# Hybrid layer on one core: the last attention pair ahead of the gate in program order, and half of the gate ahead of the second value group

## The chip, the cores and the metric

The kernel runs on one core of a Trainium2 chip. The metric is device time in microseconds of one launch; several launches are timed, and their median counts. TensorE (PE) multiplies matrices, VectorE (DVE), ScalarE (ACT) and GpSimd (POOL) do elementwise work, and SyncE (SP) issues most of the DMAs.

## The reference

One residual layer over 1024 tokens of width 1024, all in float32. A single projection feeds two groups of heads that run beside each other; their outputs are joined, projected and added to the input, and a mixture of 16 experts follows.

```python
xn = rms_norm(h, attn_norm[l])
u = xn @ w_in[l]
o_a = hgrn2_mixer(u[..., o0:o1], u[..., o1:o2], u[..., o2:o3], u[..., o3:o4], lb_all[l], hg_norm[l])
o_b = fox_mixer(u[..., o4:o5], u[..., o5:o6], u[..., o6:o7], u[..., o7:IN_COLS], fox_f_bias[l], fox_norm[l])
h = h + jnp.concatenate([o_a, o_b], axis=-1) @ w_out[l]
h = h + hier_moe(rms_norm(h, ffn_norm[l]), ...)
return rms_norm(h, final_norm)
```

`hgrn2_mixer` is a gated linear recurrence with 4 heads of width 128; its output is normalized and multiplied by `silu(g_raw)`, the gate that this change moves. `fox_mixer` is causal softmax attention with a cumulative forget bias, 8 heads of width 64.

## The kernel before, in words

Every float32 product is made of three matmuls of rounded halves (`mm3`, lines 248 to 251): hi by hi, lo by hi, hi by lo. The lo half is what the rounding to the hi half left over. ACT makes the hi half by a cast, and DVE or POOL the lo half by a subtraction.

The mixer is written out by hand as a list of calls, and a scheduler then sets each engine's order. It takes an instruction as soon as its inputs are ready by its own estimate, and among several the one that comes first in program order. So a call that is written later is a filler: its matmuls go where the earlier call leaves the engine free. What it puts out is a fixed order for each engine, and on the chip an engine waits at an instruction that is not ready, with all that is queued behind it.

The calls are these. `hg_v(p)` projects the values of two recurrent heads, `hg_fq(h)` their forget gates and queries, and `hg_core(h)` is the recurrence: seven levels of small score matmuls (line 504), with DVE and POOL work between them (lines 507 to 523). `fox_v(g)` projects the attention values of four heads, two pairs (192 matmuls of 128x256 for the second group). `fox_kq(p)` projects keys and queries of pair p, one projection each. `fox_core(p)` runs `fox_steps(p)`, a generator: for each of four blocks of 256 queries and both heads it makes two rows of scores (`row`: lines 379 to 383 on PE, the reduction L384 on DVE, the exponential L388 on ACT) and then attends over the block before (`attend`: the transposes L401, the cast `ph` L406 on ACT, the subtraction `pl` L407 on DVE, the matmuls L411 and L412). `collect` copies the sum out (L432), transposes it (L435) and reduces it (L437); after every second block `finish` normalizes four token tiles with small DVE operations (L115 to L121, L420 to L423) and two POOL multiplications (L419, L426), and stores them to `o_d` (L427).

`hg_g(p)` projects one half of the gate: 192 matmuls of 128x256, for each of 8 token tiles a tanh on ACT (L571), a product on DVE (L572) and a store to `g_d` (L573). Its tile `sg` has two buffers, so the third tanh waits for the first store. `piece` loads a stretch of `w_in`.

In program order pair 3 ends the mixer: `hg_core(3)`, `hg_g(0)`, then 18 of the 36 steps of pair 3, then `hg_g(1)`, and then the other 18 steps by hand between parts of the output projection. `prep(k)` (L621, L622) splits one of eight slices of the output weights; its target lies where the normalized input `XH`, `XL` was, so it can begin only when the last gate matmul has read that. `front_a(i)` loads one tile of mixer output (`om` from `o_d`) and gate (`gm`, or `he` for the first tile), multiplies them (L636), transposes (L642) and splits them (L645, L646). `front_parts(i)` is a generator over the 48 matmuls of one output tile (`bk<-wohi,ohi`), with an addition L666 behind each half. Two limits hold the order there: each `prep` cast is issued after the last `ph` cast written so far (`LF['act']`), and three groups of three output matmuls of tile 0 each after the last attention transpose written so far (`LF['tr']`). Then follow routing (`back`) and the experts.

Of the kernel before, what the change touches and what calls it, by code (L numbers as in the profile page):

```python
# [80 lines left out]
def build(ctx, tc, x, attn_norm, w_in, hg_lb_logits, hg_norm, fox_f_bias, fox_norm, w_out, ffn_norm,  # L81
# [197 lines left out]
    def fox_v(g):  # L279
        ts = [rtile("fv") for _ in range(4)]  # L280
        for q in range(4):
            FV[4 * g + q] = ts[q].rearrange("p (j c) -> p j c", j=NT)

        def ev(b, i):
            for q in range(4):
                v = FV[4 * g + q][:, i]
                A.copy(v[:, 0:64], b[:, q * 64:(q + 1) * 64])
                V.tensor_sub(v[:, 64:128], b[:, q * 64:(q + 1) * 64], v[:, 0:64].bitcast(F32))
            if not g:
                V.tensor_add(ff[:, :, i], b[:, 256:264], fb_bc)  # L290
        proj_t(3072 + 256 * g, 256 if g else 264, ev, None if g else 3584)
# [4 lines left out]
    def fox_kq(p):  # L296
        ka, kb, qa, qb, ql, qm = (rtile(n) for n in ("ka", "kb", "qa", "qb", "ql", "qm"))
        kl = up.tile([128, S], F32R, name="kl", tag="L", bufs=4)

        lo_, up_ = slice(0, 64), slice(64, 128)  # L300

        def ev_k(b, sl):
            for hi, h, o in ((ka, lo_, up_), (kb, up_, lo_)):
                A.copy(hi[h, sl], b[h])
                V.tensor_sub(kl[h, sl], b[h], hi[h, sl].bitcast(F32))  # L305
                mv(hi[o, sl], kl[h, sl])

        def ev_q(b, sl):
            for hi, lo, h, o in ((qa, ql, lo_, up_), (qb, qm, up_, lo_)):
                A.activation(hi[h, sl], b[h], AF.Copy, scale=-0.125)  # L310
                mv(hi[o, sl], hi[h, sl])
                V.scalar_tensor_tensor(lo[h, sl], b[h], -0.125, hi[h, sl].bitcast(F32), op0=OP.mult, op1=OP.subtract)
                mv(lo[o, sl], lo[h, sl])
        proj_c(2560 + 128 * p, ev_k)
        proj_c(2048 + 128 * p, ev_q)
        out = (((qa, ka), (ql, ka)), ((qb, kb), (qm, kb)))
        FS[p] = out
# [32 lines left out]
    LF = {}  # L350
# [107 lines left out]
    def fox_core(p):  # L458
        for _ in fox_steps(p):
            pass  # L460
# [13 lines left out]
    def hg_fq(h):  # L474
        F, K, Q = utile("hF"), utile("hK"), utile("hQ")
        HF[h], HK[h], HQ[h] = F, K, Q

        def ev_f(b, sl):
            A.activation(F[:, sl], b, AF.Tanh, scale=0.5)
            G.tensor_scalar(F[:, sl], F[:, sl], lb[:, 1, h:h + 1], lb[:, 0, h:h + 1], op0=OP.mult, op1=OP.add)  # L480
            G.tensor_scalar(K[:, sl], F[:, sl], -0.5, 0.5, op0=OP.mult, op1=OP.add)

        def ev_q(b, sl):
            A.activation(Q[:, sl], b, AF.Tanh, scale=0.5)
            V.scalar_tensor_tensor(Q[:, sl], Q[:, sl], 1.0, b, op0=OP.add, op1=OP.mult)

        proj_c(512 + 128 * h, ev_f)
        proj_c(128 * h, ev_q)
# [79 lines left out]
    def hg_g(p):  # L568
        def ev(b, i):
            z = up.tile([128, 256], F32, name="sg", tag="sg", bufs=2)  # L570
            A.activation(z, b[:, 0:256], AF.Tanh, scale=0.5)  # L571
            V.scalar_tensor_tensor(z, z, 1.0, b[:, 0:256], op0=OP.add, op1=OP.mult)  # L572
            nc.sync.dma_start(g_d[i * 128:(i + 1) * 128, 256 * p:256 * p + 256], z)  # L573
        proj_t(1536 + 256 * p, 256, ev)
# [12 lines left out]
    fox_core(1)  # L587
    hg_v(1)
    hg_core(2)
    fox_v(1)  # L590
    fox_kq(2)
    fox_core(2)
    hg_fq(3)
    fox_kq(3)
    hg_core(3)
    hg_g(0)
    steps = fox_steps(3)
    for _ in range(18):
        next(steps, None)
    hg_g(1)  # L600
    w_out_v = w_out.rearrange("l (k p) c -> p (l k) c", p=128)
    raws = []
# [13 lines left out]
            WOH.append(wh_[:, k])  # L616
            WOL.append(wl_[:, k])

    def prep(k, lim=True):
        with (tc.issue_after(LF['act'].ins) if lim else nullcontext()):  # L620
            A.copy(WOH[k], raws[k])  # L621
        (G, V)[k in (2, 5)].tensor_sub(WOL[k], raws[k], WOH[k].bitcast(F32))  # L622

    oa_cm = tc.tile_pool(name="oa", bufs=2, reuse_waits="tile")
# [45 lines left out]
        for _ in front_parts(i):  # L670
            pass

    next(steps, None)
    next(steps, None)
    prep(0)
    next(steps, None)
    next(steps, None)
    prep(1)
    next(steps, None)
    prep(2)  # L680
    next(steps, None)
    next(steps, None)
    prep(3)
    next(steps, None)
    front_a(0)
    front_a(1)
    prep(4)
    next(steps, None)
    next(steps, None)
    prep(5)  # L690
    next(steps, None)
    prep(6)
    next(steps, None)
    next(steps, None)
    prep(7)
    next(steps, None)
    next(steps, None)
    next(steps, None)
    fr0 = front_parts(0)
    with tc.issue_after(LF['tr'].ins):  # L700
        for _ in range(3):
            next(fr0, None)
    next(steps, None)
    with tc.issue_after(LF['tr'].ins):
        for _ in range(3):
            next(fr0, None)
    next(steps, None)
    with tc.issue_after(LF['tr'].ins):
        for _ in range(3):
            next(fr0, None)  # L710
    for _ in steps:
        pass
    for _ in fr0:
        pass
    ps_cm.__exit__(None, None, None)
    ps_cm = tc.tile_pool(name="pt", bufs=1, space=PSUM, reuse_waits="tile")
    ps = ps_cm.__enter__()
# [636 lines left out]
```

## Time and profile before

| | us |
|---|---|
| median of 3 runs | 1112.72 |
| lowest and highest of the runs | 1109.21, 1117.45 |
| the profiled execution, its own time | 1116.4 |
| its span, first to last instruction | 1114.6 |
| PE busy in the span | 1050.8 |
| DVE busy | 684.8 |
| ACT busy | 499.5 |
| POOL busy | 366.9 |

The profiled execution lies 3.7 us above the median of the runs, and 1.8 us of it are outside its span. Pair 0 of the attention begins at 133 us of the span, pair 1 at 261, pair 2 at 381 and pair 3 at 483; the gate's last matmul is at 544.7, and routing begins at about 601. A busy PE says little by itself: matmuls overlap, and at half clock the same work fills twice the time. So the granted clock is read beside it.

### The profile page before, as it was taken

To read this page: it belongs to the slowest core of one execution; us is meant where nothing else is said; L and a number is where in the kernel's file an instruction comes from. 1 tells how busy PE (TensorE), PEld (TensorE's weight loads), DVE (VectorE), ACT (ScalarE), POOL (GpSimd) and SP (SyncE) were. 2 spreads that over 40 slices of the span, in tenths; PEclk is the share of its full clock that TensorE was granted. 3 is DMA by queue.
4 is the path that set the end of the run, shared out by engine and by line. 5 is a ranking of instruction groups with operands and counts; after the bars stand their busy time and mean duration, and the time that the engine had idled before them with its cause. 6 is when DMAs were issued, how large, how long until landed. Compare 5 with 4: busy or idle time off the path is not lost. (4 is left out here: it accounts for less than half of the span.)

```text
span 1114.6 us, 19354 instructions
## 1 busy us (share of the span) xinstructions
PE 1050.8 (94%) x7471; PEld 891.2 (80%) x7471; DVE 684.8 (61%) x1616; ACT 499.5 (45%) x861; POOL 366.9 (33%) x283
## 2 busy tenths in 40 slices
PE   6999999989999999899899899699999999999994
PEld 6989788869988887789777788576777778878793
DVE  4537546655575546844654576656778778777445
ACT  5423343324443333424441233465666667667341
POOL 2024123221032112410322233334655456545312
PEclk8999999989999998999979999699999999999998
DMA  7120611112121410281307942369989999999974
GB/s 243 39 58 21 151 41 48 58 38 76 31 66 30 123 48 20 62 250 40 122 30 235 361 167 76 120 225 374 370 315 329 347 322 377 298 319 374 305 285 167
DMA packets 103967, 193.98 MB, mean 174 GB/s; under 512 B 9852, under 2 KB 43756, under 8 KB 103872
## 3 DMA queue, kind: packets, MB, share of 16 engines
q1 hardware_dynamic: 92576, 169.98, 43.9%
q0 software_dynamic: 7568, 20.96, 7.5%
q10 hardware_dynamic: 3728, 1.77, 0.6%
q8 instruction: 60, 0.98, 0.4%
q14 instruction: 35, 0.29, 0.1%
HBM read 155.85 MB, written 30.68 MB: 167 GB/s over the span
## 5 line engine op out<-in xcount | busy, mean ns | idle before, releaser
L249 PE MATMUL bk<-whi,xhi 128*128 128x256 f32 (+1 forms) x384 | 112.3, 292 | 4.0 <-ACT whi L178 2.8
L1053 DVE TENSOR_TENSOR wl<-we,wh 128x1024 fp32r<-128x1024 f32 x64 | 91.9, 1445 | 35.7 <-ACT wh L1051 34.9
L251 PE MATMUL bk<-whi,xlo 128*128 128x256 f32 (+1 forms) x384 | 110.6, 288 | 0.2 <-DVE xlo L216 0.2
L250 PE MATMUL bk<-wlo,xhi 128*128 128x256 f32 (+1 forms) x384 | 109.5, 285 | 1.1 <-DVE wlo L179 1.1
L250 PE MATMUL ch<-wl,xh 128*128 128x512 f32 (+1 forms) x336 | 109.4, 326 | 0.0
L1051 ACT CAST wh<-wm 128x1024 fp32r<-128x1024 f32 x84 | 87.3, 1049 | 48.3 <-PE ch L251 45.4
L251 PE MATMUL ch<-wh,xl 128*128 128x512 f32 (+1 forms) x336 | 108.3, 324 | 0.0
L249 PE MATMUL ch<-wh,xh 128*128 128x512 f32 (+1 forms) x336 | 108.2, 329 | 0.0
L249 PE MATMUL bk<-xhi,whi 128*128 128x512 f32 x256 | 104.0, 406 | 2.6 <-DVE kl L305 2.4
L1051 ACT CAST wh<-we 128x1024 fp32r<-128x1024 f32 x84 | 87.2, 1049 | 41.2 <-PE ch L251 41.0
L1053 DVE TENSOR_TENSOR wl<-wm,wh 128x1024 fp32r<-128x1024 f32 x63 | 92.9, 1504 | 17.4 <-ACT wh L1051 17.4
L251 PE MATMUL bk<-xhi,wlo 128*128 128x512 f32 x256 | 103.4, 404 | 0.0
L250 PE MATMUL bk<-xlo,whi 128*128 128x512 f32 x256 | 102.8, 401 | 0.0
L249 PEld LDWEIGHTS bk<-whi,xhi 128*128 128x128 f32 x384 | 73.1, 190 | 5.7 <-ACT whi L178 3.1
L406 ACT CAST ph<-ch 128x512 fp32r<-128x512 f32 (+1 forms) x80 | 43.1, 542 | 75.9 <-PE ch L401 75.7
L1053 POOL TENSOR_TENSOR wl<-we,wh 128x1024 fp32r<-128x1024 f32 x20 | 51.1, 2553 | 73.7 <-ACT wh L1051 73.7
L250 PEld LDWEIGHTS bk<-wlo,xhi 128*128 128x128 f32 x384 | 73.4, 191 | 1.8 <-DVE wlo L179 1.6
L251 PEld LDWEIGHTS bk<-whi,xlo 128*128 128x128 f32 x384 | 73.3, 191 | 0.7 <-DVE xlo L216 0.4
L250 PEld LDWEIGHTS ch<-wl,xh 128*128 128x128 f32 x336 | 64.9, 193 | 9.1 <-issue 4.1
L249 PEld LDWEIGHTS ch<-wh,xh 128*128 128x128 f32 x336 | 64.5, 194 | 8.0 <-ACT xh L1065 1.6
L407 DVE TENSOR_TENSOR pl<-ch,ph 128x512 fp32r<-128x512 f32 (+1 forms) x80 | 50.3, 633 | 33.3 <-ACT ph L406 33.2
L1053 POOL TENSOR_TENSOR wl<-wm,wh 128x1024 fp32r<-128x1024 f32 x21 | 52.0, 2476 | 53.7 <-ACT wh L1051 53.6
(423 smaller groups left out, 2639.6 us busy)
## 6 DMA issues: line engine op xcount, KB each, us to landing
we<-in_w_gate_dram SPq DMA_DIRECT2D x8, 2048.0 KB, 20.0
we<-in_w_up_dram SPq DMA_DIRECT2D x8, 2048.0 KB, 18.3
we<-in_w_down_dram SPq DMA_DIRECT2D x8, 2048.0 KB, 17.9
wm<-in_w_gate_dram SPq DMA_DIRECT2D x8, 2048.0 KB, 8.3
wm<-in_w_up_dram SPq DMA_DIRECT2D x8, 2048.0 KB, 10.9
wm<-in_w_down_dram SPq DMA_DIRECT2D x8, 2048.0 KB, 14.7
wraw<-in_w_in_dram SPq DMA_DIRECT2D x26, 512.0 KB, 4.3
xt<-in_x_dram SPq DMA_DIRECT2D x8, 512.0 KB, 14.8
```

The lines of the kernel that those rows point to most:

```text
L249: T.matmul(o, l[0], r[0], start=first, stop=False)
L250: T.matmul(o, l[0], r[1], start=False, stop=False)
L251: T.matmul(o, l[1], r[0], start=False, stop=last)
L406: LF['act'] = A.copy(ph[:, :o], b[:, :o])
L407: V.tensor_sub(pl[:, :o], b[:, :o], ph[:, :o].bitcast(F32))
L1051: A.copy(hi, src)
L1053: (G if j % 3 == 2 else V).tensor_sub(lo, src, hi.bitcast(F32))
```

## The change

Four things move in the list of calls, and no computation is added or taken away. The gate's first half `hg_g(0)` goes from behind `hg_core(3)` up to the place ahead of `fox_v(1)`. `hg_core(3)` goes ahead of `fox_kq(3)`. All 36 steps of pair 3 go ahead of `hg_g(1)`, as a plain `fox_core(3)`. And the hand-made end goes: the eight `prep` calls, `front_a(0)`, `front_a(1)` and `front_b(0)` simply follow, with no limits on when they are issued. Lines behind 590 move up by 3, and from the end of `prep` on by 3 and later by 40.

```diff
     hg_core(2)
+    hg_g(0)
     fox_v(1)
     fox_kq(2)
     fox_core(2)
     hg_fq(3)
+    hg_core(3)
     fox_kq(3)
-    hg_core(3)
-    hg_g(0)
-    steps = fox_steps(3)
-    for _ in range(18):
-        next(steps, None)
+    fox_core(3)
     hg_g(1)
...
-    def prep(k, lim=True):
-        with (tc.issue_after(LF['act'].ins) if lim else nullcontext()):
-            A.copy(WOH[k], raws[k])
+    def prep(k):
+        A.copy(WOH[k], raws[k])
         (G, V)[k in (2, 5)].tensor_sub(WOL[k], raws[k], WOH[k].bitcast(F32))
...
-    next(steps, None)
-    next(steps, None)
-    prep(0)
...
+    for k in range(8):
+        prep(k)
     front_a(0)
     front_a(1)
...
-    fr0 = front_parts(0)
-    with tc.issue_after(LF['tr'].ins):
-        for _ in range(3):
-            next(fr0, None)
-    next(steps, None)
...
+    front_b(0)
```

On ACT, behind the gate's last tanh (L571), the casts of the output weights (`wohi`) stand between the attention's exponentials (`Lg,fls`) and casts (`ph`). Before, from the last tanh:

```order
L571 ACTIVATE sg<-bk 128x256
L406 CAST ph<-ch 128x512
L621 CAST wohi_5704<-woraw 128x1024
L406 CAST ph<-ch 128x384
L621 CAST wohi_5704<-woraw 128x1024 x2
L406 CAST ph<-ch 128x512
L388 ACTIVATE Lg,fls<-Lg,mn 128x896
L406 CAST ph<-ch 128x512
L621 CAST wohi_5704<-woraw 128x1024
L645 ACTIVATE ohi<-bk,hgn 128x512
L645 ACTIVATE ohi<-bk,fxn 128x512
L388 ACTIVATE Lg,fls<-Lg,mn 128x1024
```

and now, from the same tanh:

```order
L571 ACTIVATE sg<-bk 128x256
L618 CAST wohi_5969<-woraw 128x1024 x4
L618 CAST wohi_5971<-woraw 128x1024 x2
L388 ACTIVATE Lg,fls<-Lg,mn 128x640
L406 CAST ph<-ch 128x512
L618 CAST wohi_5971<-woraw 128x1024 x2
L406 CAST ph<-ch 128x384
L388 ACTIVATE Lg,fls<-Lg,mn 128x768
L388 ACTIVATE Lg,fls<-Lg,mn 128x896
L388 ACTIVATE Lg,fls<-Lg,mn 128x1024
```

Six casts now stand in one run ahead of the next exponential, and the multiplications' split of `front_a(0)` (`ohi`) stands behind the last exponential, further down.

On PE, in the last steps of pair 3, `bk<-wohi,ohi` are the output matmuls of tile 0, `ub` the attention's sums. Before, in the middle of the last attention blocks:

```order
L251 MATMUL bk<-wohi_5704,olo 128x512
L411 MATMUL ub<-ph,fv 128x256
L412 MATMUL ub<-pl,fv 128x256
L411 MATMUL ub<-ph,fv 128x256
L412 MATMUL ub<-pl,fv 128x256
L401 MATMUL ch<-cft,Lg 128x128 x4
L249 MATMUL bk<-wohi_5704,ohi 128x512
L250 MATMUL bk<-wolo_5705,ohi 128x512
L251 MATMUL bk<-wohi_5704,olo 128x512
```

and now, at their very end:

```order
L411 MATMUL ub<-ph,fv 128x256
L412 MATMUL ub<-pl,fv 128x256
L411 MATMUL ub<-ph,fv 128x128
L412 MATMUL ub<-pl,fv 128x128
L435 MATMUL ch<-cft,ut 128x128 x4
L639 MATMUL bk<-cft,om 128x128 x8
L249 MATMUL bk<-wohi_5969,ohi 128x512
L250 MATMUL bk<-wolo_5970,ohi 128x512
```

The output matmuls stood between the attention's last blocks; now they stand behind all of them, behind the collect (`ch<-cft,ut`) and behind the transposes of `front_a(1)` (L639, before L642).

On PE, in pair 2, `hc<-hQ,hK` are the scores of `hg_core(3)` and `bk<-xhi,whi` and its like the first projection of `fox_kq(3)`. Before, the last projection matmuls and the first scores:

```order
L249 MATMUL bk<-xhi_75,whi 128x512
L250 MATMUL bk<-xlo_76,whi 128x512
L251 MATMUL bk<-xhi_75,wlo 128x512
L504 MATMUL hc<-hQ,hK 64x64 x12
L435 MATMUL ch<-cft,ut 128x128 x4
L401 MATMUL ch<-cft,Lg 128x128 x4
L504 MATMUL hc<-hQ,hK 64x64 x4
L411 MATMUL ub<-ph,fv 128x256
L401 MATMUL ch<-cft,Lg 128x128 x4
L504 MATMUL hc<-hQ,hK 64x64 x16
```

and now, where the first 8 scores are through:

```order
L401 MATMUL ch<-cft,Lg 128x128 x3
L379 MATMUL rb<-kb,qb 128x512
L381 MATMUL rb<-kb,qm 128x512
L504 MATMUL hc<-hQ,hK 64x64 x7
L250 MATMUL bk<-xlo_74,whi 128x512
L251 MATMUL bk<-xhi_73,wlo 128x512
L379 MATMUL rb<-kb,qb 128x128
L381 MATMUL rb<-kb,qm 128x128
L383 MATMUL rb<-mskr,idr 128x128
L249 MATMUL bk<-xhi_73,whi 128x512
```

The first set of 16 scores now stands inside the projection, where it stood behind it. On DVE, which the rows don't show, two subtractions of output weights and nine small operations of `finish` now stand between the reductions L384 right behind the gate's last tanh; the multiplication of `front_a(0)` (`om<-om,he`) stands behind the last L384, and that of `front_a(1)` behind the last reduction L420.

## Rows read from the trace of the kernel before

**Rows 1.** The page: the span, and TensorE's granted clock in 40 slices
```profile
span 1114.6 us, 19354 instructions
...
PEclk8999999989999998999979999699999999999998
```

**Rows 2.** Busy time in five stretches: us busy (instructions), PEclk, DMA share, GB/s
```profile
core 0: us, PE busy (x) PEld busy (x) DVE busy (x) ACT busy (x) POOL busy (x), PEclk, DMA share, GB/s
261.00:298.00 37.00, 37.00 (x310) 36.53 (x309) 17.81 (x57) 17.84 (x48) 4.71 (x6) 1.00 0.16 44
...
427.00:472.00 45.00, 38.61 (x418) 32.72 (x417) 40.00 (x88) 19.56 (x36) 19.71 (x21) 0.92 0.16 48
483.00:545.00 62.00, 60.79 (x509) 59.97 (x508) 29.38 (x95) 22.66 (x53) 5.58 (x6) 1.00 0.39 123
545.00:589.00 44.00, 36.54 (x196) 30.80 (x194) 26.60 (x44) 22.81 (x36) 14.21 (x6) 0.84 0.26 84
589.00:601.00 12.00, 11.34 (x50) 8.93 (x48) 4.80 (x22) 0.00 (x0) 3.13 (x4) 1.00 0.53 128
```

**Rows 3.** Timeline of PE, the gate's last matmuls: start, us, what, waits
```profile
542.82 0.28 PE L250 MATMUL bk<-wlo,xhi 128*128 128x256 f32 x1
...
544.70 0.28 PE L251 MATMUL bk<-whi,xlo 128*128 128x256 f32 x1
```

**Rows 4.** Timeline of PE, two waits behind the gate
```profile
552.55 1.09 PE L642 MATMUL bk<-cft,om 128*128 128x128 f32 x8 [2.61 <-DVE om L636]
...
556.64 0.44 PE L379 MATMUL rb<-kb,qb 128*128 128x384 f32 x1 [2.41 <-DVE mn L384]
```

**Rows 5.** Timeline of DVE in the last stretch
```profile
549.73 2.77 DVE L636 TENSOR_TENSOR om<-om,he 128x512 f32<-128x512 f32 x1 [1.05 <-DMA he<-g_d]
...
553.03 2.89 DVE L622 TENSOR_TENSOR wolo<-woraw,wohi 128x1024 fp32r<-128x1024 f32 x1
...
563.76 1.21 DVE L622 TENSOR_TENSOR wolo<-woraw,wohi 128x1024 fp32r<-128x1024 f32 x1
```

**Rows 6.** Timeline of POOL in the same stretch
```profile
541.10 1.04 POOL L426 TENSOR_TENSOR OF<-OF,fls 128x512 f32<-128x512 f32 x1 [5.13 <-DVE fls L121]
547.24 4.70 POOL L622 TENSOR_TENSOR wolo<-woraw,wohi 128x1024 fp32r<-128x1024 f32 x2 [5.10 <-ACT wohi L621]
```

**Rows 7.** Timeline of SP's queue and its loads at pair 3's start
```profile
480.82 3.20 SPq L605 DMA_DIRECT2D woraw<-in_w_out_dram  x5
...
490.33 0.33 SPq L573 DMA_DIRECT2D g_d<-sg  x1
```

**Rows 8.** Timeline of ACT there
```profile
498.97 0.38 ACT L571 ACTIVATE sg<-bk 128x256 f32<-128x256 f32 x1 [6.33 <-DMA g_d<-sg]
```

**Rows 9.** Timeline of ACT: output weights' casts, last exponential, last casts
```profile
547.46 2.00 ACT L621 CAST wohi<-woraw 128x1024 fp32r<-128x1024 f32 x2
...
565.88 1.16 ACT L388 ACTIVATE Lg<-Lg,mn 128x1024 f32<-128x1024 f32 x1
...
571.36 0.59 ACT L406 CAST ph<-ch 128x512 fp32r<-128x512 f32 x1 [1.25 <-PE ch L401]
...
574.98 0.59 ACT L406 CAST ph<-ch 128x512 fp32r<-128x512 f32 x1 [0.57 <-PE ch L401]
```

**Rows 10.** Timeline of PE around the first output tile's projection
```profile
574.70 0.49 PE L249 MATMUL bk<-wohi,ohi 128*128 128x512 f32 x1
...
588.57 0.60 PE L435 MATMUL ch<-cft,ut 128*128 128x128 f32 x4
589.51 0.50 PE L249 MATMUL bk<-wohi,ohi 128*128 128x512 f32 x1 [0.35 <-DVE he L666]
```

**Rows 11.** Timeline of DVE after the last collect
```profile
589.37 0.75 DVE L437 TENSOR_REDUCE OF<-ch 128x128 f32<-128x256 f32 x2
591.34 0.69 DVE L420 TENSOR_REDUCE fls<-fsq 128x8 f32<-128x512 f32 x1 [1.22 <-POOL fsq L419]
```

**Rows 12.** Group of DVE, 427 to 472: busy us, mean ns, idle
```profile
L508 DVE TENSOR_TENSOR hQ<-hQ,hF 128x1024 f32<-128x1024 f32 x1 | 1.8, 1781 | 0.0
```

More of the change, by code (lines that the diff above doesn't have):

```diff
@@ L671, in front_b @@
             pass
-    next(steps, None)
-    next(steps, None)
-    prep(0)
-    next(steps, None)
[L677 to L684, printed above, removed]
+    for k in range(8):
+        prep(k)
     front_a(0)
     front_a(1)
[L687 to L698, printed above, removed]
-    fr0 = front_parts(0)
-    with tc.issue_after(LF['tr'].ins):
-        for _ in range(3):
-            next(fr0, None)
[L703 to L714, printed above, removed]
+    front_b(0)
     ps_cm.__exit__(None, None, None)
```

## The prediction

> **What bounds the kernel now.** I read the page first: the span is 1114.6 us, and TensorE's granted clock is high in most slices, with a few low ones [rows 1]. So PE sets the end nearly everywhere, and a change of order can only gain or lose where PE waits or where its clock falls. Since the change moves work between stretches of the mixer, I then read the busy times by stretch [rows 2]. In the first half of pair 1 (261 to 298 us) PE is busy all of 37.0 us at full clock. In the first half of pair 3 (483 to 545), which holds both halves of the gate, it is busy 60.8 of 62.0. Both are bound by matmuls. Two stretches are not. In the second half of pair 2 (427 to 472) DVE is busy 40.0 of 45.0 and PE 38.6 at a mean clock of 0.92: DVE's work sets the pace. In the tail behind the gate (545 to 589) PE is busy 36.5 of 44.0 at a mean clock of 0.84. A mean of 0.84 between full and half speed is (1 - 0.84) x 2 x 44 = 14 us at 1.2 GHz. Here nothing is full: ACT has 22.8 us of work and DVE 26.6. This is a chain of scores, reduction, exponential, transposes, cast and sums, and PE waits for it. The prediction hangs on these two stretches.
>
> **The first part: half of the gate changes places with the second value group.** Each is 192 matmuls of 128x256. The gate's last 17 start from 542.82 to 544.70, so one takes (544.70 - 542.82) / 16 = 0.1175 us [rows 3], and 192 take 22.6. Beside pair 1's end the gate's half stands where the values stood, with the same count of matmuls: no difference. The values then run by themselves ahead of pair 2, which moves all of pair 2 back by 22.6 us, and pair 3 has 22.6 us less to cover: 62.0 - 22.6 = 39.4 us for its first half. These cancel if 39.4 us are enough for the chain. Pair 1's first half is the test: it holds 192 matmuls of one projection beside the same attention steps, and takes 37.0 [rows 2]. So I could give 2.4 us back, but pair 3 has something that pair 1 lacks. Its gate products leave through `g_d`, and the first store is issued at 490.33, behind output weights of which the first five loads alone are issued from 480.82 on [rows 7]. The third tanh waited 6.33 us for it, and ran at 498.97 [rows 8]. Before, PE had whole gate tiles queued and hardly noticed. Now attention steps stand between the gate's matmuls, and a `ph` cast stands right behind that tanh. But the third tanh also comes later by itself: two tiles beside attention steps take longer than two tiles alone, so that I take some 2.5 us of the wait as seen by PE. Sum of this part: 0, with -2.4 as the lower end and +6.3 (all of the wait) as the upper.
>
> **The second part: the recurrence core ahead of the last keys and queries.** One set of 16 scores of seven moves from behind the first projection into it. Behind the first set stands the product L508, 1.8 us on DVE [rows 12], which is then done while PE is covered by a projection; with the sum of 40.0 in 45.0 us, DVE time taken out shortens the stretch about one for one. Gain 2 us, 4 if the second set's work follows it. Against it: the core's last matmuls stood among the second projection and the start of pair 3, and now stand ahead of that projection, with state updates of DVE between them. I take 1 us for them. Sum -1 us, from -4 to +1.
>
> **The third part: the tail.** Its start is the gate's last matmul at 544.7 [rows 3], and the same attention steps are left then as before: five rows' ends and three attention blocks of head 0, then all the rest. I go through it in order.
>
> Up to the last exponential the old kernel takes 565.88 + 1.16 - 544.7 = 22.3 us [rows 9]. In it PE waited 2.61 us for the product of `front_a(0)` and then 2.41 us for a reduction that was queued behind it on DVE [rows 4]. Both go, since that product now stands behind the last reduction: -5. New is the run of six casts on ACT, ahead of an exponential that is ready: two such casts take 2.00 us [rows 9], six take 6. Five of the eight subtractions come at once on POOL, two of them take 4.70 us [rows 6], five 11.8. DVE's part beside them grows: a subtraction of output weights took 2.89 us while POOL was at its own, and 1.21 otherwise [rows 5], 1.7 us more. DVE has two such subtractions and nine small operations of `finish` between the last reductions; ACT's run and DVE's waits lie largely beside each other, so I take 3 us of both, with 0 (all beside) and 5 x 1.7 = 8.5 (one wait for each POOL subtraction) as ends. That gives 22.3 - 5 + 3 = 20.3.
>
> The Trainium skill, SBUF — State Buffer, section Who interferes with whom, says that a VectorE instruction with two inputs in SBUF and a GpSimd instruction that reads SBUF exclude each other for the whole of an instruction. The trace agrees (2.89 against 1.21 us). By that rule alone each POOL subtraction of 2.35 us could hold one DVE operation, 11.8 us in place of the 3 that I take.
>
> `finish` of the first half now ends late: its last product on POOL stands behind five subtractions, so at 12 to 15 us after the gate's end. From the end of that product before, at 541.10 + 1.04 = 542.14 [rows 6], to the start of the product of `front_a(0)` at 549.73 [rows 5], store, load and landing took 7.6 us. So that product can start only at 20 to 23 us, and in DVE's order the last collects and subtractions stand behind it. I take 2.7 us beyond the 20.3: 23.
>
> Then come eight attention blocks, which follow each other in (574.98 - 571.36) / 3 = 1.21 us [rows 9]; one is begun by then, seven take 8.5: 31.5. Before, from 574.70 to 588.57 the last of these blocks were spread between the 48 matmuls of output tile 0 [rows 10], and PE worked on one while the other waited. Now all 48 stand behind the last block, the collect, and the transposes of `front_a(1)`. Collect: copy and transposes, about 1.6. Then DVE: from 588.57, when the collect's transposes begin [rows 10], to the end of the reduction L420 at 591.34 + 0.69 = 592.03 [rows 11] it takes 3.5 us, of which 0.6 is counted. The product of `front_a(1)` stands behind that reduction, 0.7, and its transposes take 1.1 (8 in the row at 552.55 [rows 4]): 31.5 + 1.6 + 2.9 + 0.7 + 1.1 = 37.8. The 48 matmuls then take 11.3 us, as those of the next tile did in 589 to 601 [rows 2]: 49.1. An addition of some 1 us stands before anything new: 50.1. The old kernel was there at 589.51 [rows 10], 44.8 us behind the gate. So the tail grows by 5.3 us. The cover that goes is 11.3 us of output matmuls; 5 us come back from the waits that go.
>
> **The rest.** Routing and experts keep their order within the scheduler's freedom: routing of tile 0 comes ahead of output tile 1 and no longer behind it, with the same matmuls. I cost this at nothing; the experts' matmuls cover it, and if that cover is thin it costs the 0.35 us with which PE waited for that addition [rows 10].
>
> **Sum.** 0 - 1 + 5.3 = +4.3 us. The profiled execution took 1116.4, so the same one would take 1120.7; against the median of the runs, 1112.7, the forecast is 1117.0 us. A measurement of this kernel tells about 1% (11 us) from no change, so this counts as no change. Bounds: first part -2.4 to +6.3, second -4 to +1, tail from -2 (nothing for casts and waits, nor for the late product) to +11.
>
> **Rivals.**
>
> The clock in the tail. Before, 14 us of it ran at 1.2 GHz, after PE's waits of 2.6 and 2.4 us. If it falls again and stays low while PE waits 4 to 5 us in the collect, the 48 matmuls run at half speed for much of their time: up to 11.3 us more, I take 9. Then 4.3 + 9 = 13.3, 1126 us. For it: attention blocks alone leave PE half idle. Against it: the wait comes once, and two waits stood there before.
>
> DVE behind POOL. The nine small operations and both subtractions each wait for a POOL subtraction: 8.5 us from rows in place of 3, 5.5 more, and 1122.5 us. (The page of the Trainium skill named above, SBUF — State Buffer, section Who interferes with whom, would have it so.) For it: the product L636 took 2.77 us beside POOL [rows 5]. Against it: ACT's casts delay the same steps anyway.
>
> The first store of the gate. All of the 6.33 us is seen by PE, since attention casts stand behind the tanh, and the blocks behind wait too: 3.8 us more than I take, 1121 us. For it: the same loads are issued at the same place. Against it: a later third tanh.
>
> Faster. Pair 2 is bound by DVE; if the early scores draw the whole core forward, its second half loses 6 us (its PE work of 38.6 us is the floor), and the two waits of 5 us in the tail go, with the half-clock time that followed them (14 us at half speed, 7 us lost). If the new queue on ACT costs no more than it did, that is 4.3 - 5 - 7 = -8, 1105 us. It decides from the point where the first exponential behind the gate is not later than before. For it: 5 + 7 us stand in the rows. Against it: 11.3 us of cover are gone whatever the clock does.
>
> **Chances.** The forecast 0.50, the clock 0.23, DVE behind POOL 0.10, the first store 0.07, faster 0.10. Over 1% slower (from 1124): 0.19 of the clock's 0.23, and 0.02 each of the forecast, POOL and the store, 0.25 together. Over 1% faster (below 1102): 0.05 of the last. Within 1%: 0.70. The range leaves out about one in ten on either side: 1106 to 1128 us.
>
> **What would show it.** In the new profile: the values run alone for some 22.6 us ahead of pair 2; pair 3's first half takes 37 to 43 us; a run of six casts follows the last tanh; the first output matmul starts some 38 us behind the gate's last one; POOL's subtractions stand in a row, with DVE's beside them over 2 us. Wrong would be a tail shorter than 44 us up to the end of the first output tile, a low clock through the output matmuls, or a first half of pair 3 with waits of more than 5 us.

## The result, and the profile after

The changed kernel takes 1121.22 us (median; 1118.44 to 1124.06), beside 1111.29 us for the kernel before in the same measurement. The ratio is 1.0089, with a 95% interval from 1.0075 to 1.0104: slower, by a little under 1%. The prediction said 1117.0 us, a range of 1106 to 1128, and 0.70 for "within 1%". The profiled execution took 1124.06 us, 7.7 us more than that of before (1116.4).

The page answers [rows 1]:

```profile
span 1122.3 us, 19351 instructions
...
PEclk8999999989999999999878999799999999999997
```

One slice is 28 us. The low digit in the middle of the mixer (an 8, in pair 2) is gone, and behind the gate there are three low ones (8, 7, 8) in place of one 7. The windows say how much. They have the columns of [rows 2]; the first and the third stretch are the ones of [rows 2] where they now lie, the others are chosen by events: the values alone; pair 3 up to the gate's last matmul; from the gate's last matmul to the first output matmul; from the gate's last matmul to the end of output tile 0; and the rest of the output projection.

```profile
262.00:299.00 37.00, 37.00 (x310) 36.55 (x308) 17.94 (x57) 17.79 (x48) 4.69 (x6) 1.00 0.16 44
354.50:386.50 32.00, 30.08 (x245) 29.91 (x244) 16.53 (x77) 10.29 (x35) 4.17 (x4) 0.95 0.20 54
456.00:501.00 45.00, 38.38 (x418) 33.57 (x417) 39.27 (x103) 20.03 (x36) 21.39 (x22) 1.00 0.12 38
511.00:545.60 34.60, 34.60 (x289) 34.16 (x288) 16.67 (x49) 14.96 (x38) 2.44 (x3) 1.00 0.51 168
545.60:593.40 47.80, 30.14 (x155) 24.24 (x153) 35.96 (x75) 24.86 (x40) 16.05 (x8) 0.75 0.18 62
545.60:607.70 62.10, 44.38 (x220) 36.12 (x218) 39.78 (x87) 25.62 (x41) 18.13 (x11) 0.78 0.38 119
607.70:715.60 107.90, 107.46 (x607) 92.41 (x604) 64.19 (x330) 34.58 (x72) 31.92 (x22) 1.00 0.54 191
```

For the kernel before, the last two of these stretches, bounded by the same events:

```profile
544.70:589.50 44.80, 37.01 (x199) 31.10 (x197) 27.10 (x45) 22.81 (x36) 14.21 (x6) 0.85 0.26 83
589.50:706.70 117.20, 112.15 (x620) 96.24 (x620) 74.86 (x354) 35.84 (x72) 36.30 (x26) 0.98 0.58 205
```

The gate's last matmul is at 545.5 us, where it was at 544.7 [rows 3]: all that the change moved ahead of it sums to nothing. From there to the end of output tile 0 it takes 62.2 us in place of 44.8, 17.4 more. The rest of the output projection and routing takes 107.9 in place of 117.2, 9.3 less: PE has no idle time left there (107.46 of 107.90), and 13 of its matmuls have moved ahead. So the place of the loss is the tail, and up to half of the loss there is given back behind it. Some 2.5 of the 9.3 us may belong to this one execution of before, at a mean clock of 0.98: e3 and e4 below, with the same order there, take 114.8 and 114.7 us at 1.00.

What stands in the tail is seen on three engines. PE, in answer to [rows 4] and [rows 10]:

```profile
545.47 0.28 PE L251 MATMUL bk<-whi,xlo 128*128 128x256 f32 x1
...
547.93 0.39 PE L381 MATMUL rb<-ka,ql 128*128 128x512 f32 x1
550.12 0.44 PE L379 MATMUL rb<-ka,qa 128*128 128x384 f32 x1 [1.80 <-DVE mn L384]
...
554.90 0.80 PE L379 MATMUL rb<-ka,qa 128*128 128x512 f32 x1 [4.11 <-DVE mn L384]
...
560.52 0.79 PE L379 MATMUL rb<-ka,qa 128*128 128x512 f32 x1 [4.39 <-DVE mn L384]
...
590.78 1.97 PE L639 MATMUL bk<-cft,om 128*128 128x128 f32 x8 [3.43 <-DVE om L633]
593.46 0.80 PE L249 MATMUL bk<-wohi,ohi 128*128 128x512 f32 x1 [0.71 <-DVE olo L643]
```

PE waits 10.3 us (1.80 + 4.11 + 4.39) for the reductions of scores, where such waits of 2.41 and 0.31 us stood before. DVE and POOL, in answer to [rows 5] and [rows 6], show why the reductions were late:

```profile
547.19 11.65 POOL L619 TENSOR_TENSOR wolo<-woraw,wohi 128x1024 fp32r<-128x1024 f32 x5 [1.64 <-ACT wohi L618]
547.45 2.15 DVE L115 TENSOR_SCALAR fls<-fls 128x8 f32<-128x8 f32 x1
549.58 0.47 DVE L384 CUSTOM_DVE_ANT_0 Lg<-rb,Gt,mn 128x256 f32<-128x256 f32 x1
549.99 1.94 DVE L117 TENSOR_SCALAR fls<-fls 128x8 int32<-128x8 int32 x1
551.96 2.28 DVE L119 TENSOR_TENSOR fls<-fls 128x8 f32<-128x8 f32 x1
554.16 0.68 DVE L384 CUSTOM_DVE_ANT_0 Lg<-rb,Gt 128x512 f32<-128x512 f32 x1
554.77 1.80 DVE L120 TENSOR_TENSOR fls<-fls 128x8 f32<-128x8 f32 x1
556.49 3.43 DVE L619 TENSOR_TENSOR wolo<-woraw,wohi 128x1024 fp32r<-128x1024 f32 x1
559.85 0.60 DVE L384 CUSTOM_DVE_ANT_0 Lg<-rb,Gt,mn 128x384 f32<-128x384 f32 x1
```

While POOL does its five subtractions without a break, five DVE instructions take 2.15 + 1.94 + 2.28 + 1.80 + 3.43 = 11.6 us. The four small ones each end about where a subtraction of POOL ends (one each 2.33 us from 547.19 on); the last, itself a subtraction of output weights, ends 1.1 us behind POOL's fifth. Their like take 0.16 us, and 1.22 the last, when POOL is idle: so 9.7 us of DVE's time are lost. The reductions L384 between them are not slowed (0.68 us), but they are queued behind. ACT, in answer to [rows 9]. Of the kernel before, these are the three exponentials ahead of the one shown there:

```profile
549.83 1.05 ACT L388 ACTIVATE Lg<-Lg,mn 128x896 f32<-128x896 f32 x1
556.62 1.15 ACT L388 ACTIVATE Lg<-Lg,mn 128x1024 f32<-128x1024 f32 x1 [2.11 <-DVE mn L384]
560.62 1.04 ACT L388 ACTIVATE Lg<-Lg,mn 128x896 f32<-128x896 f32 x1
```

and after:

```profile
546.07 5.77 ACT L618 CAST wohi<-woraw 128x1024 fp32r<-128x1024 f32 x6
551.74 0.83 ACT L388 ACTIVATE Lg<-Lg,mn 128x640 f32<-128x640 f32 x1
...
555.30 0.94 ACT L388 ACTIVATE Lg<-Lg,mn 128x768 f32<-128x768 f32 x1
...
560.50 1.04 ACT L388 ACTIVATE Lg<-Lg,mn 128x896 f32<-128x896 f32 x1 [4.16 <-DVE mn L384]
...
562.67 1.15 ACT L388 ACTIVATE Lg<-Lg,mn 128x1024 f32<-128x1024 f32 x1 [1.04 <-DVE mn L384]
...
571.70 1.04 ACT L388 ACTIVATE Lg<-Lg,mn 128x896 f32<-128x896 f32 x1 [0.49 <-DVE mn L384]
...
574.09 1.15 ACT L388 ACTIVATE Lg<-Lg,mn 128x1024 f32<-128x1024 f32 x1
```

Six exponentials stand behind the gate's end; before there were four. The gate's last matmul comes at the same time, but two rows of the attention are not yet through their exponentials by then.

### The profile page after: what moved, and what is told of

Its sections match the earlier page's. It is cut to its first block, busy times and chain, and to the rows that moved or that the text cites. A ratio compares the mean times of both kernels' runs of the same rounds, so it can differ in the third digit from the quotient of the medians.

```text
span 1122.3 us, 19351 instructions
## 1 busy us (share of the span) xinstructions
PE 1051.5 (94%) x7471; PEld 891.5 (79%) x7471; DVE 681.0 (61%) x1616; ACT 500.3 (45%) x861; POOL 365.4 (33%) x283
## 5 line engine op out<-in xcount | busy, mean ns | idle before, releaser
L388 ACT ACTIVATE Lg<-Lg,mn 128x128 f32<-128x128 f32 (+3 forms) x64 | 49.7, 777 | 57.4 <-DVE mn L384 47.5
L407 DVE TENSOR_TENSOR pl<-ch,ph 128x512 fp32r<-128x512 f32 (+1 forms) x80 | 50.3, 633 | 33.5 <-ACT ph L406 33.3
```

What stands on the lines that cost most here:

```text
L388: A.activation(L[:, :nb * 128], L[:, :nb * 128], AF.Exp, scale=-1.0, bias=prev, accum_out=fl[:, 0, i, hh:hh + 1])
L407: V.tensor_sub(pl[:, :o], b[:, :o], ph[:, :o].bitcast(F32))
```

## The experiments

Each kernel was timed beside the kernel before. The letters of the theories are explained in the expectations, and change from group to group. The table gives the measured ratio to the kernel before, and three stretches in us from the profiled execution of each (one only; the runs of the kernel before lie up to 0.8% apart, so a difference of 2 us in a stretch tells little): from the end of the 192 matmuls beside pair 1 to the gate's last matmul, from there to the end of output tile 0, and on to the last matmul of the output tiles.

| run | ratio [95%] | to the gate's end | to the end of tile 0 | rest |
|---|---|---|---|---|
| before | 1 | 191.2 | 44.8 | 117.2 |
| after | 1.0089 [1.0075, 1.0104] | 191.1 | 62.2 | 107.9 |
| e1 swap alone | 1.0093 [1.0071, 1.0115] | 194.2 | 48.5 | 115.3 |
| e2 swap undone | 1.0025 [1.0009, 1.0040] | 200.5 | 47.3 | 107.8 |
| e3 core first alone | 1.0004 [0.9987, 1.0021] | 195.4 | 45.1 | 114.8 |
| e4 tail undone | 1.0016 [0.9998, 1.0034] | 190.3 | 46.5 | 114.7 |
| e5 no POOL subtractions | 1.0035 [1.0011, 1.0059] | 191.2 | 58.5 | 107.9 |
| e6 output between | 1.0087 [1.0060, 1.0114] | 190.8 | 58.2 | 111.1 |
| e7 both | 1.0061 [1.0039, 1.0083] | 190.9 | 51.5 | 112.6 |
| e8 both, no swap | 1.0022 [1.0003, 1.0041] | 203.3 | 40.4 | 111.8 |
| e9 filled waits | 1.0054 [1.0040, 1.0069] | 190.9 | 60.2 | 107.9 |
| e12 old tail, no POOL | 0.9996 [0.9975, 1.0017] | 189.5 | 44.9 | 113.3 |

The comparison of the two traces puts the loss in the tail; whether the tail's new order makes it, or what the other two parts left for the tail, it does not say. The first four runs take the change apart.

**e1, the swap alone.**

```diff
+    hg_g(0)
     fox_v(1)
...
     hg_core(3)
-    hg_g(0)
```

> The old kernel with the gate's first half moved ahead of the second value group, and nothing else moved: 18 steps of pair 3, the gate's second half and the hand-made end stay. Theory A (the loss is in the tail; the values alone cost only what pair 3 gives back): within 4 us of the old kernel; the values alone take about 32 us ahead of pair 2 in place of 22.6, pair 3's first half is about 27 us shorter, and the first output matmul stays some 30 us behind the gate's last one. Theory B (the loss is the values that run alone and wait for their evacuation): 6 to 10 us slower than the old kernel, with the tail as before.

Measured: 1120.35 us, as slow as the whole change, though the tail is the hand-made one: theory B's time. The profiled execution shows 3.0 us more ahead of the gate's end and 3.7 us more up to the end of tile 0. One wait ahead of the second projection of `fox_kq(3)` is 3.15 us; in e4, where `hg_core(3)` goes first, it is 1.71 at the same place.

```profile
496.95 0.79 PE L249 MATMUL bk<-xhi,whi 128*128 128x512 f32 x1 [3.15 <-DVE kl L305]
```

**e2, the swap undone.**

```diff
-    hg_g(0)
     fox_v(1)
...
     fox_kq(3)
+    hg_g(0)
     fox_core(3)
```

> The changed kernel with the gate's first half put back behind pair 3's keys and queries; pair 3's steps still all stand ahead of the gate's second half, and the end is plain. Theory A: most of the loss stays, 6 to 10 us slower than the old kernel, with PE waits of together 8 to 12 us on the reductions behind the gate and the first output matmul 45 us or more behind the gate's last one. Theory B: within 3 us of the old kernel.

Measured: 1114.18 us, theory B's time too. With both halves of the gate beside pair 3 the gate ends 9 us later, but only one exponential is left behind its last tanh:

```profile
553.68 3.88 ACT L618 CAST wohi<-woraw 128x1024 fp32r<-128x1024 f32 x4
557.46 1.15 ACT L388 ACTIVATE Lg<-Lg,mn 128x1024 f32<-128x1024 f32 x1
```

The new tail then costs 47.3 us, not 62.2.

**e3, the core first, alone.**

```diff
     hg_fq(3)
+    hg_core(3)
     fox_kq(3)
-    hg_core(3)
```

> The old kernel with only the recurrence core of head 3 ahead of pair 3's keys and queries. Both theories: 1 to 4 us faster than the old kernel or no difference; pair 2's second half loses 2 us or so, and the tail is as before. A loss of over 3 us would mean that the core's end ahead of the keys and queries is a cost of its own.

Measured: 1111.13 us, no change.

**e4, the tail undone.** The swap and the core first stay; the 18 steps, the limits and the interleaved end of the kernel before come back.

```diff
     fox_kq(3)
-    fox_core(3)
+    steps = fox_steps(3)
+    for _ in range(18):
+        next(steps, None)
     hg_g(1)
...
```

> The changed kernel with the old end: 18 steps of pair 3, the gate's second half, and then the 18 other steps by hand between the weight casts and output matmuls, with their limits. Theory A: the loss goes, within 4 us of the old kernel. Theory B: the loss stays, 6 to 10 us slower than the old kernel. If the parts add up, the difference to the old kernel is the sum of those of the swap alone and of the core alone.

Measured: 1113.14 us, as theory A had it; so neither theory is right alone. Here, too, six exponentials stand behind the gate, but the tail takes 46.5 us. The parts don't add: the new tail costs 0.73% on top of the swap (after against e4) and 0.21% without it (e2 against e3); the swap costs 0.64% with the new tail (after against e2) and 0.12%, which can't be told from nothing, with the old one, if the core goes first (e4 against e3). With the core first, as in the change, the loss is made where the two meet: attention rows that the swap leaves behind the gate, in the tail's new order. That the swap without the core first (e1) loses as much in the old tail is another thing, and stays open. What of the new order makes the loss, the next four ask.

**e5, all subtractions of output weights on DVE.**

```diff
-        (G, V)[k in (2, 5)].tensor_sub(WOL[k], raws[k], WOH[k].bitcast(F32))
+        V.tensor_sub(WOL[k], raws[k], WOH[k].bitcast(F32))
```

> The changed kernel with all eight subtractions of output weights on DVE and none on POOL; nothing else is edited. In the changed kernel's trace PE waits 1.80, 4.11 and 4.39 us for reductions L384 behind the gate's last matmul, and DVE's small operations of finish take 1.8 to 3.4 us each while five POOL subtractions run. Theory B (DVE held up by POOL's subtractions is a main part of the loss): these waits fall to 1 to 2 us each although DVE gets five subtractions of some 1.2 us more, the last exponential comes 21 to 24 us behind the gate's last matmul instead of 29.6, the stretch from there to the end of the first output tile goes from 62.2 to 54 to 57 us, and the time is 1114 to 1117 us. Theory A (only the order counts: the output matmuls stand behind the last attention block): the waits stay, since DVE's own five subtractions take their place, and the time is 1120 to 1123 us.

Measured: 1115.33 us; the ratio falls by 0.54%, some 6 us, although DVE has five more subtractions to do. PE's waits at the same places:

```profile
547.51 0.44 PE L379 MATMUL rb<-ka,qa 128*128 128x384 f32 x1 [0.95 <-DVE mn L384]
...
549.26 0.55 PE L379 MATMUL rb<-ka,qa 128*128 128x512 f32 x1 [1.08 <-DVE mn L384]
...
553.27 0.79 PE L379 MATMUL rb<-ka,qa 128*128 128x512 f32 x1 [1.27 <-DVE mn L384]
```

They sum to 3.3 us instead of 10.3, and on DVE the small operations are short again:

```profile
546.83 0.16 DVE L115 TENSOR_SCALAR fls<-fls 128x8 f32<-128x8 f32 x1
```

This is as theory B had it, in the waits, in the last exponential (23.6 us behind the gate, 29.8 in the changed kernel) and in the time. The stretch to the end of tile 0, 58.5 us, is a little over its 54 to 57.

**e6, output matmuls between the last blocks.**

```diff
     front_a(0)
-    front_a(1)
     front_b(0)
+    front_a(1)
```

> The changed kernel with front_a(1) written behind front_b(0) instead of ahead of it; nothing else is edited. The scheduler then puts 12 of the 48 output matmuls of tile 0 or some more between the last attention blocks and no transposes of front_a(1) ahead of them. Theory A (lost cover): the first output matmul starts 8 to 12 us earlier than the 47.9 us behind the gate's last matmul, the first output tile ends some 54 us behind the gate instead of 62.2, the routing keeps most of its gain, and the time is 1113 to 1117 us. Theory B: PE's waits of 10.3 us for reductions L384 lie ahead of all this and stay, the blocks behind go at DVE's and ACT's pace, and the time is 1118 to 1122 us.

Measured: 1120.15 us, nothing gained. The first output matmul came 15.7 us earlier behind the gate (32.3 us, not 48.0), as theory A had it, but not the time. The output matmuls came in long runs between the blocks. ACT waited twice over 5 us for the next block's transposes, so that tile 1's product, which DVE does behind the last block, came late, and PE waited the same 3.42 us for it, now behind tile 0:

```profile
582.29 1.02 ACT L406 CAST ph<-ch 128x384 fp32r<-128x384 f32 x2 [5.74 <-PE ch L401]
...
598.06 1.97 PE L639 MATMUL bk<-cft,om 128*128 128x128 f32 x8 [3.42 <-DVE om L633]
601.60 0.80 PE L249 MATMUL bk<-wohi,ohi 128*128 128x512 f32 x1 [1.56 <-DVE olo L643]
```

4.0 us are won up to there, and 3.2 are lost again in the rest. So output matmuls at this place gain nothing. That doesn't clear lost cover, on which the prediction's tail rested. In e4 the last exponential ends 29.8 us behind the gate's last matmul (541.78), as late as in the changed kernel, but tile 0 ends 16.7 us after it and not 32.4:

```profile
570.45 1.16 ACT L388 ACTIVATE Lg<-Lg,mn 128x1024 f32<-128x1024 f32 x1
```

```profile
588.30 0.50 PE L249 MATMUL bk<-wohi,ohi 128*128 128x512 f32 x1 [0.35 <-DVE he L666]
```

Four blocks and the end of a fifth, not eight, stand behind that exponential there; tile 1's product is done before them, and the output matmuls run between them from 573.50 on. So the whole difference of the two tails, 15.7 us, lies behind the last exponential. No run changes this cover alone.

**e7, both edits.**

> Both edits together: all subtractions of output weights on DVE, and front_a(1) behind front_b(0). If A and B both hold and add, the stretch behind the gate falls to 46 to 50 us, routing stays near 108 us, and the time is 1107 to 1111 us, a little under the kernel before. If only one of them holds, the time is that of the better of the two single edits, 1113 to 1117 us.

The edits are those of e5 and e6. Measured: 1116.50 us, not better than e5 alone; the two did not add, though the tail is 7 us shorter than in e5: 4.7 us of that are lost again in the rest.

**e8, both edits and the swap undone.** The edits are those of e2, e5 and e6.

> The same two edits, and the gate's first half back behind fox_kq(3), so that both halves of the gate cover pair 3's steps and only one exponential instead of six stands behind the gate's last tanh. In the run with the swap undone PE waited 5.69 us for the product om of front_a(0), whose input is stored by finish behind POOL's five subtractions. Theory (few attention steps left behind the gate are worth more than values that cover pair 1): that wait falls to 1 to 3 us, output matmuls stand among the last blocks, and the time is 1106 to 1110 us, below both kernels and below the run with both edits alone by 1 to 4 us. Rival (the place of the gate's half does not matter once the tail is right): the same time as the run with both edits within 1.5 us.

Measured: 1112.64 us, a ratio of 1.0022. Without the swap it is 0.39% below e7, as the theory had it, but not below the kernel before, and no better than e2. The wait of 5.69 us that the expectation starts from fell only to 3.69, and its reason was misread: in e2 the mixer output was stored at 540.24, well ahead, and the product stood on DVE behind a subtraction that waited for ACT, and was then held by POOL:

```profile
558.15 2.84 DVE L633 TENSOR_TENSOR om<-om,he 128x512 f32<-128x512 f32 x1
```

In e8's profiled execution the tail is 6.9 us shorter than in e2, but 2.8 us more stand ahead of the gate's end and 4.0 in the rest. What POOL's subtractions cost without the swap no run tells by itself.

**e9, e10, e11: the clock.** The windows say that much of the tail runs at 1.2 GHz (a mean of 0.78, against 0.85 before). Is that a cause? The same lines, at other places in the three kernels, fill PE's waits with matmuls that nobody reads:

```diff
+    def fill(after, n):
+        f = hbank()
+        with tc.issue_after(after.ins):
+            for _ in range(n):
+                T.matmul(f[:, 0:128], ident, ident, start=True, stop=True)
...
+                if p == 3:
+                    fill(lm, FILL.get((i, hh, k), 0))
```

> The changed kernel with 51 more matmuls of 128x128 into a PSUM bank that nothing reads, issued on PE right ahead of its four long waits behind the gate: 5 ahead of the wait of 1.80 us, 16 ahead of each of the two of 4.11 and 4.39 us for reductions L384, and 14 ahead of the one of 3.43 us for the product om. At full clock such a matmul takes 0.21 us, as the first ones of the kernel do, so they take 1.1, 3.4, 3.4 and 3.0 us and end inside the waits. Nothing else is edited. Theory C (most of the loss is the granted clock that falls behind these waits): the half-speed stretches of 20.5 and 6.8 us behind the gate go or shrink to under 7 us together, the stretch from the gate's last matmul to the end of the first output tile falls from 62.2 to 49 to 54 us, and the time is 1108 to 1114 us, though work was added. Theory D (the waits are the loss, the clock only reports them): the stretch stays at 61 to 64 us and the time at 1120 to 1124 us.

Measured: 1117.03 us, between the two theories. In the trace (a matmul of this kind leaves two records, and seven of them take 1.48 us at full clock, 0.21 each) 16 of the fillers came one wait too late, and 16 more stand between attention sums:

```profile
548.06 1.28 PE L358 MATMUL hc<-cft 128*128 128x128 f32 x10
550.03 0.44 PE L387 MATMUL rb<-ka,qa 128*128 128x384 f32 x1 [0.69 <-DVE mn L394]
...
554.81 0.79 PE L387 MATMUL rb<-ka,qa 128*128 128x512 f32 x1 [4.11 <-DVE mn L394]
...
555.83 5.38 PE L358 MATMUL hc<-cft 128*128 128x128 f32 x32
560.97 0.48 PE L387 MATMUL rb<-ka,qa 128*128 128x512 f32 x1
```

```profile
545.50:592.90 47.40, 36.97 (x257) 32.66 (x255) 35.38 (x74) 24.70 (x40) 17.14 (x8) 0.93 0.18 64
```

The mean clock up to the first output matmul rose from 0.75 to 0.93, and the stretch went from 47.8 to 47.4 us, so the rows and blocks there hardly gained from PE's clock. The 48 output matmuls behind it gained more: 12.7 us at a clock of 1.00, not 14.3 at 0.88. Over all runs, the mean of span times (1 - clock) is 40.0 us for the changed kernel and 28.6 here: 11.4 us of low clock went, and some 4 us of time with them (0.35%). The misplaced fillers may hide up to 16 x 0.21 = 3.4 us more.

In e10 and e11 the numbers of fillers are these:

```diff
+    FILL = {(7, 0, 1): 10, (6, 1, 0): 9, (7, 1, 1): 4}
...
+                    fill(LF['tr'], FILL.get((I, hh, j0), 0))
+                    if (I, hh, j0) == (3, 0, 2):
+                        fill(LF['m1'], 16)
...
+            if p == 3 and I == 3:
+                fill(lt_, 14)
```

The first line is that of e10; the rest is e11, with 16 at `(3, 0, 2)`, where `m1` is the first of the last block group's sums and `lt_` the collect's last transpose.

> The kernel before with 23 such matmuls ahead of PE's waits behind the gate: 10 ahead of the one of 2.61 us for om, 9 ahead of the one of 2.41 us for a reduction, 4 ahead of the one of 1.13 us. Nothing else is edited. Theory C: the half-speed stretch of 13.7 us behind the gate goes or falls under 4 us, and the time is 4 to 7 us below the kernel before (a ratio of 0.994 to 0.9965). Theory D: a ratio of 0.999 to 1.003.

Measured: a ratio of 1.0013 [0.9995, 1.0032]. Nothing was gained.

> The run with both edits and without the swap, with 46 such matmuls behind the gate: 16 ahead of the wait of 3.69 us for the first product om, 16 ahead of and between the waits of 1.98 and 1.90 us for ph and pl, 14 ahead of the wait of 3.42 us for the second product om. Its two half-speed stretches there were 13.7 and 10.2 us. Theory C: they go or fall under 7 us together, and the time is 6 to 12 us below that run's 1112.6, a ratio to the kernel before of 0.992 to 0.997, the best of all. Theory D: a ratio of 1.001 to 1.005.

Measured: 1113.30 us, 1.0010 [0.9990, 1.0029]. The low clock behind the gate went (a mean of 1.00 up to the end of tile 0, where e8 has 0.77), and over all runs 7.6 us of span times (1 - clock) with it. The stretch took 39.9 us in place of 40.4, and the ratio fell by 0.12%, which can't be told from nothing. So the clock is worth some 4 us in the changed kernel and nothing measurable in the other two: low clock here is mostly what waits look like and not what makes them long.

**e12, the old tail without POOL's subtractions.** It is e4 with the edit of e5.

> The run with the tail undone (the swap and the core first, the hand-made end of the kernel before), with all eight subtractions of output weights on DVE. In that run's trace POOL's subtractions come one at a time, since the casts ahead of them are held back, and they held two small operations of finish, L117 for 1.68 us and L121 for 1.99 us in place of some 0.17. Theory B (what POOL's subtractions cost hangs on their coming in one run): only 3.3 us are to be had, of which DVE's own five subtractions take back some, and the time is 1110 to 1113 us, a ratio of 0.999 to 1.002. Rival (subtractions on POOL cost 6 us wherever attention rows are left behind the gate): 1106 to 1109 us, below both kernels.

Measured: 1108.51 us, and 0.9996 [0.9975, 1.0017], beside 1110.38 for the kernel before. The ratio is theory B's, the time nearly the rival's; the interval doesn't part them. It is the fastest version tried, and equal to the kernel before. With the subtractions off POOL in both, the new end is still 0.39% slower than the old one (e5 against e12): POOL's hold is a part of what the new order costs, not all of it. In e4's trace two operations of `finish` were held, and no wait of PE there was over 2.4 us:

```profile
545.28 2.38 POOL L622 TENSOR_TENSOR wolo<-woraw,wohi 128x1024 fp32r<-128x1024 f32 x1 [2.97 <-ACT wohi L621]
546.01 1.68 DVE L117 TENSOR_SCALAR fls<-fls 128x8 int32<-128x8 int32 x1
```

## Why the prediction was right, and where its steps were not

The forecast was no change, on the slow side: +4.3 us, where +9.9 were measured by the medians. The sign and the place (the tail) were right. The size came out of terms that were off by more, and that the time lies so near is in part luck: the tail's +17.4 is over its upper bound of +11, and the rest, costed at nothing, gave back 7 to 9 us.

- **The first part**, forecast 0: the gate's end came 0.8 us later, and the execution was 0.9 us late already at the end of the 192 matmuls beside pair 1. Both terms were off and cancelled. The values alone moved pair 2's start by 29.6 us (from 380.8 to 410.4), not 22.6: two waits of PE for DVE's part of their evacuation (L288) cost 3.2 us, and the clock fell for a while (0.95 in 354.5 to 386.5). Pair 3 then took 34.6 us up to the gate's last matmul, not 39.4, with PE busy all the time. PE did not wait for the first store of the gate, its rival; the third tanh waited 2.08 us for it, where it had waited 6.33.
- **What that step missed** is the larger thing. It asked whether PE is filled up to the gate's end and took that end for a fixed point of the chain. "The same attention steps are left then as before" is the sentence that failed: 34.6 us are enough for PE because two rows more are left for later: it holds 289 matmuls, 220 fewer than the 509 of [rows 2], and the gate's half is only 192 of them. It could be read ahead of the run, from the order of ACT: four exponentials stood behind the last tanh, now six. The rows of that order, quoted ahead of the prediction for the casts among them, show rows of 640 and 768 there that the rows of before don't have.
- **The second part**, forecast -1: pair 2 took 100.5 us in place of 102.6, and e3 measured no change. As forecast, too small to tell. That e1, with the swap and the old core order, loses what e4 does not is left open: pair 2 took 105.7 us there and 100.4 in e4, and its trace shows 3.15 us for 1.71 at one wait and lower clocks, from one execution.
- **The third part**, forecast +5.3, measured +17.4 up to the end of tile 0. The last exponential ended 29.8 us behind the gate's last matmul, not 20.3: this is the mis-sized term, by 9.5 us. The first of the two old waits went, as forecast. The second had been read wrongly: the reduction it waited for stood behind the subtraction L622 of 2.89 us [rows 5], held by POOL, and not behind the product. So that kind of wait did not go with the product, but grew from 2.41 to 10.3 us:

```profile
555.84 0.74 DVE L384 CUSTOM_DVE_ANT_0 Lg<-rb,Gt,mn 128x512 f32<-128x512 f32 x1
```

Without the hold, in e5, the last exponential ended 23.6 us behind the gate (566.17 + 1.15 - 543.71), so it is worth 6.2. Against the 17.3 us left of the old chain (22.3 - 5), 12.5 were added where 3 had been costed for DVE's waits and ACT's casts together: 6.2 are the hold (net of DVE's five more subtractions in e5), and 6.3 are left to the two rows more, costed at nothing, and the casts, which no run tells apart. The late product of `front_a(0)`, +2.7, cost nothing: at 573.95 it stood behind the last reduction anyway. The blocks took 1.27 us each, forecast 1.21. From the last block to the first output matmul it took 9 us, forecast 6.3, with the wait of 3.43 us for the product of tile 1.
- **The cover**, the reason given for the sign, held by the traces: from the last exponential to the end of tile 0 the forecast was 29.8 us (50.1 - 20.3), and 32.4 were measured, where the kernel before took 22.5. It was no more tested than that: e6 put output matmuls back between the blocks and gained nothing, since the blocks then came later.
- **The rest**, costed at nothing, gave back 9.3 us by these two executions, some 7 against e3 and e4. Before, PE had idle time there and waits of 0.9 to 1.9 us; with routing of tile 0 ahead of output tile 1, PE is full. The kernels of the table that keep the new order of the end (after, e2, e5, e9) all have 107.8 or 107.9 us there.
- **The signs.** The six casts in a run, POOL's subtractions in a row and DVE's operations of over 2 us beside them came. Pair 3's first half (34.6 us, not 37 to 43) and the first output matmul (48.0 us behind the gate, not 38) did not, and the low clock through the output matmuls, named as a sign of being wrong, came in part (0.88).
- **The rivals.** DVE behind POOL was true, with a chance of 0.10 and a price of 5.5 us over the forecast. The Trainium skill, SBUF — State Buffer, section Who interferes with whom, has two inputs in SBUF as one case, and lists `tensor_scalar` among the operations that can take the shared ports. The trace agrees with both: L119 (two inputs, 2.28 us) and L115 (one, 2.15 us) were held. L384 (0.68 us) and, in the kernel before, L407 (0.56 us at 547.59), which read one input from PSUM, were not. By that rule alone five operations wait for five subtractions, 11.8 us by the prediction's estimate; DVE lost 9.7 and the kernel 6. The clock in the tail fell as that rival said, but its price of 9 us was not found: filling the waits brought 4 us in e9, where misplaced fillers may hide 3.4 more, and nothing measurable in the other kernels of e10 and e11.

## What to carry to other kernels

When work is moved ahead of a marker such as a gate's end, count in each engine's order what stands behind the marker before and after: a stretch can be full and shorter only because it leaves a longer chain behind. A late chain costs most where nothing else is left to run behind it: e4's was as late as the changed kernel's, but had output matmuls to run meanwhile. In a chain of short DVE steps, elementwise work on POOL is not free cover; here five POOL subtractions in a row held five DVE operations, with all that was queued behind them. A low granted clock in a stretch where PE waits is a sign of the waits first; fill them before counting it as time.

## What was not expected of the hardware

A DVE instruction on 128x8 elements, 0.16 us long, took up to 2.28 us while POOL subtracted (L119), and one with a single tensor input (L115) 2.15 us. Raising the mean clock of a stretch from 0.75 to 0.93 shortened it by 0.4 us of 47.8, with 16 misplaced fillers in it.
